# One pace number of a one-core decoder layer: 11 gathered expert rows move from beside the second group's attention and output projection into the expert loop

## The chip, the core and the metric

The program runs on one core of one Trainium2 chip. A core has five engines with a queue each: TensorE (PE in the profile, its weight loads PEld), VectorE (DVE), ScalarE (ACT), GpSimd (POOL) and SyncE (SP). Each works through its own queue in the order in which the instructions stand there, and an instruction that has to wait holds up those behind it. The metric is the device time of one execution, in microseconds (us); lower is better.

## What is computed

One decoder layer on 1024 tokens of width 1024: a mixing half (four retention heads, four heads of causal differential attention, an output projection), then a mixture of 16384 tiny experts (one row of `u` and one of `v` each). Each token picks 128 of them (8 heads, 16 each):

```python
x = x + jnp.concatenate([ret_out, diff_out], axis=-1) @ w_out[l]
x = x + peer(rmsnorm(x, norm_ffn_g[l]), peer_wq[l], peer_subkeys[l], peer_u[l], peer_v[l])
...
# inside peer(), for each block of 128 tokens; e are the 8 x 16 chosen experts of a token, g their gates
ue = jnp.take(u, e, axis=0)
ve = jnp.take(v, e, axis=0)
act = jax.nn.gelu(jnp.einsum('thkd,td->thk', ue, xb), approximate=False)
return jnp.einsum('thk,thkd->td', g * act, ve)
```

## The kernel before

**Two groups of tokens.** The 1024 tokens are eight tiles of 128. Tiles 0 to 2 are the first group ("gathered": `GROUPS[0]`), tiles 3 to 7 the second ("dense"). Both go through `front`: projections, retention and attention by head, output projection, the expert router. Then the experts are done in two ways.

**The dense way**, for the five tiles of the second group: every token meets all 16384 experts. A loop over 32 groups `g` of 4 blocks `e` of 128 experts takes the products with `u` (`experts_in`, lines 740 to 742, PSUM tiles `psH`), GELU, the multiplication by the gates (line 830), the split of the result into a high and a low half (`wh` line 834 on ScalarE, `wl` line 836 on VectorE), the split of `v` (`vh` line 840, `vl` line 842), and the products with `v` (lines 818 to 820). Ten output pieces (tile, half) are summed: four stay in PSUM for the whole loop (`kp0` to `kp3`), six come out of two rotating banks `psV` once a group and are added by VectorE (line 854, `accl`, `accd`, `accS`, `accc_intra`, `accab`, `accpack`, in this order). The `u` products of 39 of the 128 blocks (`SPILL`) are made earlier, beside the router, and stored. After the loop each dense tile is finished: lines 862 and 864 bring its halves together, `finish` squares (line 799, ScalarE), takes the root, and scales (line 801, `fin`).

**The gathered way**, for the three tiles of the first group: per tile 128 rows of `u` (one expert for each token, line 891, an indirect DMA issued by GpSimd into a buffer `ug`), each multiplied with the tokens and summed by VectorE (line 893); then GELU and gates (`shs`, lines 894 and 895); then 128 rows of `v` (line 898, buffer `vg`), each scaled and added into `sa` by VectorE (line 900); then `finish` (`sfin`). That makes 768 rows. The first tile has 5 buffers, which a gather may only refill when VectorE is through with the row that is in it; the later tiles have 7 (line 884 and on, `row`).

**What sets the order.** The gathered rows are written last in the program. A scheduler that models time while it builds puts each engine's queue together, and would take the rows wherever VectorE looks free. `gate` ties the n-th row's VectorE step behind an instruction of the list `gates`; the list is filled by `gated`, which adds `PER` entries (1.5 here) at every step of the generator that it paces:

```python
def gated(g, per):
    due = 0.0
    for y in g:
        due += per[y == "turned"]
        while due >= 1.0:
            gates.append(last_dve())
            due -= 1.0
        yield y
...
run(gated(weave(until(gd, "routing"), sparse_routes(sp, lates, s0, sn, ug, ug, ug), ROUTE, 1), PER[:2]))
```

The paced stretch is the second group's attention with retention, its output projection and the norm behind it, up to the mark "routing". Its 83 steps give 124 entries. Beside the second router and the building of the dense gates (`dense_routes`) `PER[2]` is 0 and no row is let in. The last entry is added at the first gate multiplication (line 830) of the loop: all other rows are free from there on.

Of the kernel before, what the change touches and what calls it, by code (L numbers as in the profile page):

```python
# [56 lines left out]
SPILL = 39  # L57
PACE = (8, 3)
SLOW = 4
PER = (1.5, 1.5, 0.0)  # L60
NC2 = 80
TC = {"schedule_with_timeline_sim": True}

# [36 lines left out]
def layer_kernel(ctx, tc, x, wt, wn, wo, wq, sk, ut, u, v, gmix, gffn, gfin, gsub, dlam, consts, alb, out):  # L100
# [450 lines left out]
    def sparse_routes(rp, late, g0, nt, *rooms):  # L551

        gates_of(rp, late, nt, rooms[0])
        for lt in range(nt):
            t = ST.index(g0 + lt)
            V.tensor_copy(gA[t].rearrange("p (h k) -> p h k", h=PH), late.cv[:, lt])
            i1, i2 = decode(rp, late, lt, *rooms)
            V.scalar_tensor_tensor(i1, i1, float(NK), i2, op0=ALU.mult, op1=ALU.add)
            V.tensor_copy(idxA[t].rearrange("p (h k) -> p h k", h=PH), i1)
            yield  # L560

    def dense_routes(rp, gp, pp, late):

        before = None
        gates_of(rp, late, ND, ("mz", 1))
        for t in range(ND):
            i1, i2 = decode(rp, late, t)
            ps = pp.tile([P, 4, P], F32, tag="B", bufs=2, name="psR")
            for c, src in enumerate((i2, i1, late.cv[:, t])):
                PE.transpose(ps[:, c], src.rearrange("p h k -> p (h k)"), ident)  # L570
            r = rp.tile([P, P // 8, 4, 8], F16, tag="rt", bufs=2, name="rt")
            by = ps.rearrange("p c (q t) -> p q c t", t=8)
            A.activation(r[:, :, 0:2], by[:, :, 0:2], AF.Copy)
            A.activation(r[:, :, 2], by[:, :, 2], AF.Copy, scale=GS)
            V.scalar_tensor_tensor(r[:, :, 3], by[:, :, 2], GS, r[:, :, 2], op0=ALU.mult, op1=ALU.subtract)
            lo = rp.tile([P, P // 8, 8], F32, tag="rl", bufs=2, name="rl")
            if ACTS:
                A.activation(lo, r[:, :, 3], AF.Copy)
            if before is not None:
                yield from build_g(gp, pp, *before)  # L580
            else:
                yield
            before = r, lo, t
        yield from build_g(gp, pp, *before)
# [82 lines left out]
    def pool(name, es=ctx, **kw):  # L667
        return es.enter_context(tc.tile_pool(name=name, bufs=1, reuse_waits="tile", **kw))

    def weave(a, b, na=1, nb=1):  # L670

        i = j = 0
        while a is not None or b is not None:
            if b is None or (a is not None and i * nb <= j * na):
                i += 1
                try:
                    yield next(a)
                except StopIteration:
                    a = None
            else:  # L680
                j += 1
                try:
                    yield next(b)
                except StopIteration:
                    b = None
# [7 lines left out]
# [10 lines that stand above are left out]
    def run(g):  # L703
        for _ in g:
            pass

    def until(g, mark):
        for y in g:
            if y == mark:
                return  # L710
            yield y
# [36 lines left out]
    def spills(pf):  # L748
        for i, ei in enumerate(early):
            two = pf.tile([P, 2, 512], F32, tag="A", bufs=2, name="psHs")  # L750
            SY.dma_start(hs_d[i], experts_in(ei, lambda hf: two[:, hf]))
            yield

    with ExitStack() as es:
# [19 lines left out]
        with ExitStack() as e2:  # L774
            fd = pool("fd", e2)
            md.tp = md.ap = md.fp = fd
            md.big = (fd, "big", BIGS)
            run(gated(weave(until(gd, "routing"), sparse_routes(sp, lates, s0, sn, ug, ug, ug), ROUTE, 1), PER[:2]))
            gh = spills(pf)
            run(weave(gd, islice(gh, 16 // SLOW), SLOW, 1))  # L780
        gp = pool("gp", es)
        run(gated(weave(dense_routes(gp, gp, pf, late), gh, *PACE), (PER[2], 0)))

# [156 lines left out]
```

## Time and profile before

| | us |
|---|---|
| median of 3 runs (2809.43 to 2814.86) | 2811.94 |
| the profiled execution, whole | 2812.24 |
| its span, first to last instruction | 2810.5 |
| around the span | 1.7 |

| stretch of the span | us | what runs |
|---|---|---|
| second group's attention with rows beside it | 445 to 680 | head 0 to 3 |
| output projection, norm, rows beside it | 680 to 803 | |
| router, dense gates, 39 early blocks | 803 to 1260 | no rows |
| change to the loop | 1260 to 1296 | |
| expert loop, with all other rows | 1296 to 2803 | 32 groups |
| last finishes | to 2810.5 | |

A timeline row gives the start, the duration, engine and line, the operation with output and inputs, and in brackets how long the engine had been idle and what ended that. The stretches were taken from the rows of the trace; the busy time of the engines in them is the first group of rows below.

### The profile page before, as it was taken

The page shows a single profiled execution, that of the slowest core. Times are in us where ns is not written, and L with a number is a line of the kernel's source. Part 1 is how long each engine was busy: PE and PEld are TensorE (multiplying, and loading weights), DVE is VectorE, ACT ScalarE, POOL GpSimd, SP SyncE. Part 2 cuts the span into 40 slices and gives each one's busy share as a digit, 9 for nine tenths or more (in the row PEclk, how much of TensorE's full clock was granted, in tenths as well). Part 3 has the DMA queues.
Part 4 walks back from the last instruction along what each step waited for, and adds up shares of the span by engine and source line. Part 5 has one row for each costly group of instructions (what it writes and reads, how often), then busy time and mean ns, then how long its engine had stood idle before and what let it go on. Part 6 is the DMA issues. An engine that isn't in the chain of part 4 may idle for free.

```text
span 2810.5 us, 43147 instructions
## 1 busy us (share of the span) xinstructions
PE 2681.3 (95%) x16043; PEld 2421.6 (86%) x16043; DVE 2303.7 (82%) x4496; ACT 997.4 (35%) x1879; POOL 1071.4 (38%) x782
## 2 busy tenths in 40 slices
PE   7979989888889999999999999999999999999998
PEld 6867888776789999998888888999999999899997
DVE  3554789887478989986999998888998889889987
ACT  4553335554233356772222222222222222223222
POOL 0000004543310000003555556665666567765662
PEclk9989999999989999999999999999999999999999
DMA  7546557877853347799999899898999989989995
GB/s 265 188 177 231 194 191 254 292 276 259 305 193 132 112 150 244 240 281 330 347 347 338 337 374 354 325 348 336 327 344 338 341 333 346 352 317 341 337 348 204
DMA packets 302076, 797.46 MB, mean 284 GB/s; under 512 B 25116, under 2 KB 119336, under 8 KB 297768
## 3 DMA queue, kind: packets, MB, share of 16 engines
q1 hardware_dynamic: 190120, 390.41, 39.2%
q0 software_dynamic: 111744, 404.28, 39.0%
q8 instruction: 126, 2.06, 0.3%
q14 instruction: 86, 0.70, 0.1%
HBM read 698.97 MB, written 95.62 MB: 283 GB/s over the span
## 4 chain that ended last, share of the span: by engine, by line
PE 66%; DVE 8%; DMA 5%; issue 4%; POOL 2%; ACT 1%; SPq 0%; POOLq 0%; DVEq 0%; ACTq 0%
PE psH L742 7%; PE psH L741 7%; PE psH L740 7%; PE psV L818 5%; PE psV L819 5%; PE psV L820 5%; PE kp L820 3%; PE kp L819 3%; PE kp L818 3%; PE psHs L740 3%; PE psHs L742 3%; PE psHs L741 3%; PE psG L613 3%; DVE ug L893 2%; DMA ug<-in_u,idx 2%
## 5 line engine op out<-in xcount | busy, mean ns | idle before, releaser
L891 POOL DMA_INDIRECT ug<-in_u,idx x384 | 529.9, 1380 | 903.5 <-ACT st L615 458.0
L898 POOL DMA_INDIRECT vg<-in_v,idx x384 | 536.1, 1396 | 393.8 <-DVE sa L900 289.8
L893 DVE SCALAR_TENSOR_TENSOR ug<-ug,sx 128x1024 f32<-128x1024 f32 x384 | 458.7, 1223 | 55.5 <-DMA ug<-in_u,idx 54.7
L900 DVE SCALAR_TENSOR_TENSOR sa<-vg,shs,sa 128x1024 f32<-128x1024 f32 x384 | 492.0, 1281 | 10.5 <-DMA vg<-in_v,idx 6.2
L741 PE MATMUL psH<-nl,uh 128*128 128x320 f32 x1424 | 439.5, 309 | 0.0
L740 PE MATMUL psH<-nh,uh 128*128 128x320 f32 x1424 | 439.3, 309 | 0.0
L742 PE MATMUL psH<-nh,ul 128*128 128x320 f32 x1424 | 438.3, 309 | 0.3 <-DVE ul L728 0.3
L818 PE MATMUL psV<-vh,wh 128*128 128x512 f32 x768 | 300.0, 392 | 1.1 <-DVE accl L854 1.1
L819 PE MATMUL psV<-vl,wh 128*128 128x512 f32 x768 | 299.8, 391 | 0.0
L740 PEld LDWEIGHTS psH<-nh,uh 128*128 128x128 f32 x1424 | 267.3, 188 | 5.8
L741 PEld LDWEIGHTS psH<-nl,uh 128*128 128x128 f32 x1424 | 267.3, 188 | 4.8
L742 PEld LDWEIGHTS psH<-nh,ul 128*128 128x128 f32 x1424 | 267.0, 188 | 4.3 <-DVE ul L728 0.6
L726 ACT ACTIVATE uh<-uraw 128x1024 fp32r<-128x1024 f32 x128 | 135.8, 1061 | 321.5 <-PE psH L741 218.0
L743 ACT ACTIVATE ga<-psH 128x320 f32<-128x320 f32 x178 | 75.1, 429 | 447.0 <-PE psH L742 434.2
L740 PE MATMUL psHs<-nh,uh 128*128 128x320 f32 x624 | 195.7, 315 | 6.8 <-ACT ga L743 6.8
L819 PE MATMUL kp<-vl,wh 128*128 128x512 f32 x512 | 200.1, 393 | 0.3 <-DVE vl L842 0.3
L818 PE MATMUL kp<-vh,wh 128*128 128x512 f32 x512 | 194.7, 393 | 4.7 <-ACT wh L834 4.7
L164 ACT ACTIVATE whi<-wraw 128x1024 fp32r<-128x1024 f32 x104 | 109.9, 1058 | 241.2 <-PE psT L173 124.8
L741 PE MATMUL psHs<-nl,uh 128*128 128x320 f32 x624 | 194.1, 311 | 0.0
L742 PE MATMUL psHs<-nh,ul 128*128 128x320 f32 x624 | 192.6, 313 | 0.8 <-DVE ul L728 0.8
L728 DVE TENSOR_TENSOR ul<-uraw,uh 128x1024 fp32r<-128x1024 f32 x128 | 156.9, 1226 | 44.1 <-ACT uh L726 43.9
L820 PE MATMUL psV<-vh,wl 128*128 128x512 f32 x456 | 173.3, 389 | 0.0
(251 smaller groups left out, 6036.4 us busy)
## 6 DMA issues: line engine op xcount, KB each, us to landing
uraw<-in_ut SPq DMA_DIRECT2D x128, 512.0 KB, 6.6
vraw<-in_v SPq DMA_DIRECT2D x128, 512.0 KB, 6.9
g_d<-st SPq DMA_DIRECT2D x80, 512.0 KB, 6.3
gt<-g_d SPq DMA_DIRECT2D x32, 1280.0 KB, 9.6
wl_d<-wlo SPq DMA_DIRECT2D x52, 512.0 KB, 2.9
wlo<-wl_d SPq DMA_DIRECT2D x52, 512.0 KB, 4.3
wraw<-in_wt SPq DMA_DIRECT2D x32, 512.0 KB, 4.4
wraw<-in_wq SPq DMA_DIRECT2D x32, 512.0 KB, 4.6
```

Of the source, the lines that this page charges most:

```text
L726: A.activation(uh, raw, AF.Copy)
L728: V.tensor_sub(ul, raw, uh.bitcast(F32))
L740: PE.matmul(ps, uh[:, dc], xh[:, dc, sl], start=(dc == 0), stop=False)
L741: PE.matmul(ps, uh[:, dc], xl[:, dc, sl], start=False, stop=False)
L742: PE.matmul(ps, ul[:, dc], xh[:, dc, sl], start=False, stop=(dc == DC - 1))
L818: PE.matmul(ps, Wh[e][:, sl], Vh[e][:, so], start=start, stop=False)
L819: PE.matmul(ps, Wh[e][:, sl], Vl[e][:, so], start=False, stop=False)
L820: PE.matmul(ps, Wl[e][:, sl], Vh[e][:, so], start=False, stop=stop)
L891: G.indirect_dma_start(out=ug, out_offset=None, in_=u, in_offset=bass.IndirectOffsetOnAxis(ap=idxA[t][:, k:k + 1], axis=0))
L893: gate(V.scalar_tensor_tensor(ug, ug, 1.0, xt, op0=ALU.mult, op1=ALU.mult, accum_out=hs[:, k:k + 1]))
L898: G.indirect_dma_start(out=vg, out_offset=None, in_=v, in_offset=bass.IndirectOffsetOnAxis(ap=idxA[t][:, k:k + 1], axis=0))
L900: gate(V.scalar_tensor_tensor(ac, vg, hs[:, k:k + 1], ac, op0=ALU.mult, op1=ALU.add))
```

## The change

```diff
-PER = (1.5, 1.5, 0.0)
+PER = (1.37, 1.37, 0.0)
```

The 83 steps now give 113 entries. In VectorE's queue 113 rows, not 124, stand ahead of the loop's first line 830, so the first tile enters the loop with 15 rows of `u` left, not 4. No instruction is added, removed or changed; every queue holds the same instructions in another order. The order is the same up to the first head of the second group, and again, on VectorE and TensorE, through the router and the dense gates. It differs in the paced stretch and in the loop.

In the names below a number belongs to a buffer; `qT`, `kT`, `psT` and so on are as in the code. First place: VectorE beside the attention of the second group, about the end of its first head, as one piece of the difference (- before, + after). `Z` are row maxima and sums, `rz` reciprocals, `am` the masked retention scores, `S` the retention state.

```order
 L893 SCALAR_TENSOR_TENSOR ug,shs<-ug,sx 128x1024
 L371 TENSOR_REDUCE Z<-psS 128x1
-L893 SCALAR_TENSOR_TENSOR ug,shs<-ug,sx 128x1024
 L306 SCALAR_TENSOR_TENSOR S<-S,ret 128x128
-L893 SCALAR_TENSOR_TENSOR ug,shs<-ug,sx 128x1024 x2
-L295 TENSOR_TENSOR am<-ret,c_intra 128x128
-L893 SCALAR_TENSOR_TENSOR ug,shs<-ug,sx 128x1024
-L383 RECIPROCAL rz<-Z 128x1
-L893 SCALAR_TENSOR_TENSOR ug,shs<-ug,sx 128x1024
+L893 SCALAR_TENSOR_TENSOR ug,shs<-ug,sx 128x1024 x3
+L295 TENSOR_TENSOR am<-ret,c_intra 128x128
+L893 SCALAR_TENSOR_TENSOR ug,shs<-ug,sx 128x1024
```

Single rows are taken out or close up. Between the sixth line 382 of the group (of twenty) and the first scaling behind the heads (line 415) 68 rows stand before and 59 after; the other two rows go from the projection and norm behind it.

Second place: VectorE at the start of the loop. Before:

```order
L830 TENSOR_TENSOR gl<-gl,gt 128x640
L893 SCALAR_TENSOR_TENSOR ug,shs<-ug,sx 128x1024 x2
L728 TENSOR_TENSOR ul<-uraw,uh 128x1024
L893 SCALAR_TENSOR_TENSOR ug,shs<-ug,sx 128x1024 x2
L836 TENSOR_TENSOR wls<-gl,wh 128x640
L830 TENSOR_TENSOR gl<-gl,gt 128x640
L895 TENSOR_TENSOR shs<-shs,gA_83 128x128
L900 SCALAR_TENSOR_TENSOR sa<-vg,shs,sa 128x1024
L836 TENSOR_TENSOR wls<-gl,wh 128x640
L900 SCALAR_TENSOR_TENSOR sa<-vg,shs,sa 128x1024
L830 TENSOR_TENSOR ga<-ga,gt 128x640
```

After:

```order
L830 TENSOR_TENSOR gl<-gl,gt 128x640
L893 SCALAR_TENSOR_TENSOR ug,shs<-ug,sx 128x1024 x2
L728 TENSOR_TENSOR ul<-uraw,uh 128x1024
L893 SCALAR_TENSOR_TENSOR ug,shs<-ug,sx 128x1024 x3
L836 TENSOR_TENSOR wls<-gl,wh 128x640
L830 TENSOR_TENSOR gl<-gl,gt 128x640
L893 SCALAR_TENSOR_TENSOR ug,shs<-ug,sx 128x1024 x3
L836 TENSOR_TENSOR wls<-gl,wh 128x640
L893 SCALAR_TENSOR_TENSOR ug,shs<-ug,sx 128x1024 x2
L830 TENSOR_TENSOR gl<-gl,gt 128x640
L830 TENSOR_TENSOR ga<-ga,gt 128x640
L893 SCALAR_TENSOR_TENSOR ug,shs<-ug,sx 128x1024 x2
```

Before, four rows of `u`, then rows of `v`, stand around the first `wl` splits (line 836); after, five rows of `u` stand ahead of the first, three more ahead of the second, four more ahead of the third, and three more ahead of `shs`, behind which all rows of `v` stand.

Third place: VectorE's end, from the last `wl` split of the loop on. Before:

```order
L836 TENSOR_TENSOR wl_13178<-ga,wh 128x640
L900 SCALAR_TENSOR_TENSOR sa<-vg,shs,sa 128x1024 x2
L137 RECIPROCAL rs_f<-rs_f 128x1
L801 SCALAR_TENSOR_TENSOR sfin<-sa,rs_f,gfb 128x1024
L862 TENSOR_TENSOR fa<-kp_13170,fa 128x512
L862 TENSOR_TENSOR fa<-kp_13171,fa 128x512
L854 TENSOR_TENSOR accl<-psV,accl 128x512
L854 TENSOR_TENSOR accd<-psV,accd 128x512
```

After, the beginning and the end of it:

```order
L836 TENSOR_TENSOR wl_13178<-ga,wh 128x640
L900 SCALAR_TENSOR_TENSOR sa<-vg,shs,sa 128x1024 x4
L862 TENSOR_TENSOR fa<-kp_13170,fa 128x512
L862 TENSOR_TENSOR fa<-kp_13171,fa 128x512
L854 TENSOR_TENSOR accl<-psV,accl 128x512
L900 SCALAR_TENSOR_TENSOR sa<-vg,shs,sa 128x1024
L854 TENSOR_TENSOR accd<-psV,accd 128x512
...
L137 RECIPROCAL rs_f<-rs_f 128x1
L900 SCALAR_TENSOR_TENSOR sa<-vg,shs,sa 128x1024
L801 SCALAR_TENSOR_TENSOR fin<-fa,rs_f,gfb 128x1024
L137 RECIPROCAL rs_f<-rs_f 128x1
L801 SCALAR_TENSOR_TENSOR sfin<-sa,rs_f,gfb 128x1024
```

Before, 2 rows are left there and `sfin` of the third tile comes ahead of all dense finishes. After, 15 rows are left (4 and then 11 singly between the lines 854, 862, 864 and 801), and `sfin` is the last instruction of the queue. Between the first line 830 and this place 642 rows stand before, 640 after.

## Rows read from the trace of the kernel before

**Rows 1.** Busy us (and instructions) of each engine, clock and DMA by stretch.

```profile
core 0: us, PE busy (x) PEld busy (x) DVE busy (x) ACT busy (x) POOL busy (x), PEclk, DMA share, GB/s
...
505.00:680.00 175.00, 151.28 (x961) 130.10 (x960) 143.97 (x274) 89.37 (x235) 83.80 (x72) 0.94 0.76 266
...
1380.00:2760.00 1380.00, 1377.01 (x7472) 1237.32 (x7472) 1224.55 (x1461) 352.56 (x492) 850.61 (x597) 1.00 0.92 341
```

**Rows 2.** VectorE's timeline: the combining step L382 of the shortest tile, four heads.

```profile
447.03 0.77 DVE L382 SCALAR_TENSOR_TENSOR e<-e,rz,e 128x512 f32<-128x512 f32 x1
...
508.33 0.75 DVE L382 SCALAR_TENSOR_TENSOR e<-e,rz,e 128x512 f32<-128x512 f32 x1
...
574.35 0.75 DVE L382 SCALAR_TENSOR_TENSOR e<-e,rz,e 128x512 f32<-128x512 f32 x1
...
634.48 0.75 DVE L382 SCALAR_TENSOR_TENSOR e<-e,rz,e 128x512 f32<-128x512 f32 x1
```

**Rows 3.** Waits from 505 to 680 us: total us, times, longest.

```profile
DVE ug L893 <- DMA ug<-in_u,idx: 19.9, 15, 2.9
...
PE ret L297 <- DVE am L295: 7.3, 4, 3.4
PE pov L393 <- DMA dvh<-dv_d: 5.8, 1, 5.8
```

**Rows 4.** VectorE's timeline at the loop's start: start, us, instruction, idle before.

```profile
1296.66 0.83 DVE L830 TENSOR_TENSOR gl<-gl,gt 128x640 f32<-128x640 f32 x1 [5.65 <-issue]
...
1298.55 1.22 DVE L893 SCALAR_TENSOR_TENSOR ug<-ug,sx 128x1024 f32<-128x1024 f32 x1
...
1303.12 0.82 DVE L836 TENSOR_TENSOR wls<-gl,wh 128x640 fp32r<-128x640 f32 x1
...
1306.12 0.82 DVE L836 TENSOR_TENSOR wls<-gl,wh 128x640 fp32r<-128x640 f32 x1
1306.85 1.28 DVE L900 SCALAR_TENSOR_TENSOR sa<-vg,shs,sa 128x1024 f32<-128x1024 f32 x1
...
1320.44 1.28 DVE L900 SCALAR_TENSOR_TENSOR sa<-vg,shs,sa 128x1024 f32<-128x1024 f32 x1 [2.22 <-DMA vg<-in_v,idx]
1321.64 0.68 DVE L854 TENSOR_TENSOR accl<-psV,accl 128x512 f32<-128x512 f32 x1
```

**Rows 5.** GpSimd's timeline: gathers ahead of the loop and in its first 15 us.

```profile
1260.01 0.94 POOL L891 DMA_INDIRECT ug<-in_u,idx  x1 [457.97 <-ACT st L615]
...
1298.90 1.68 POOL L898 DMA_INDIRECT vg<-in_v,idx  x1 [36.71 <-DVE ug L893]
...
1311.18 1.43 POOL L898 DMA_INDIRECT vg<-in_v,idx  x1 [0.30 <-issue]
```

**Rows 6.** TensorE's timeline at the loop's start: expert 1's last products; third psV.

```profile
1308.35 0.62 PE L820 MATMUL kp<-vh,wls 128*128 128x512 f32 x2
...
1324.63 0.39 PE L818 MATMUL psV<-vh,wh 128*128 128x512 f32 x1
```

**Rows 7.** VectorE's timeline at the end of the program.

```profile
2741.94 2.60 DVE L900 SCALAR_TENSOR_TENSOR sa<-vg,shs,sa 128x1024 f32<-128x1024 f32 x2
2744.45 0.68 DVE L854 TENSOR_TENSOR accc_intra<-psV,accc_intra 128x512 f32<-128x512 f32 x1
...
2779.64 2.60 DVE L900 SCALAR_TENSOR_TENSOR sa<-vg,shs,sa 128x1024 f32<-128x1024 f32 x2
...
2785.50 1.28 DVE L801 SCALAR_TENSOR_TENSOR sfin<-sa,rs_f,gfb 128x1024 f32<-128x1024 f32 x1 [0.27 <-DVE rs_f L137]
2786.70 1.28 DVE L862 TENSOR_TENSOR fa<-kp,fa 128x512 f32<-128x512 f32 x2
...
2803.31 0.43 DVE L864 COPY fa<-accpack 128x512 f32<-128x512 f32 x1
2805.28 0.17 DVE L137 RECIPROCAL rs_f<-rs_f 128x1 f32<-128x1 f32 x1 [1.54 <-ACT rs_f L136]
2805.48 1.28 DVE L801 SCALAR_TENSOR_TENSOR fin<-fa,rs_f,gfb 128x1024 f32<-128x1024 f32 x1
```

**Rows 8.** TensorE's timeline: the last products of kp0 and kp1.

```profile
2785.38 0.62 PE L820 MATMUL kp<-vh,wl 128*128 128x512 f32 x2
```

## The prediction

> **What bounds the kernel now.** I read the busy time by stretch first, then the waits inside the paced stretch, then VectorE's timeline at the two ends of the loop, because the change touches only VectorE's work and its order.
>
> In the loop TensorE is busy in 1377.0 of 1380 us, VectorE in 1224.6 [rows 1]. TensorE sets the pace there and VectorE has 155 us to spare. In the second group's attention neither is full: from 505 to 680 us TensorE is busy in 151.3 of 175 us, at a mean granted clock of 0.94, which is mostly the upper of its two levels, and VectorE in 144.0 [rows 1]. They alternate: VectorE stands 19.9 us still for gathered rows that have not landed, TensorE 7.3 us for the masked scores that VectorE makes, and 5.8 us for a load of `dvh` that has nothing to do with the rows [rows 3]. At the end of the program the last dense `fin` starts at 2805.48 and takes 1.28, so VectorE ends at 2806.8 [rows 7]; the rest of the span is the last store.
>
> So the change takes VectorE work out of a stretch in which VectorE matters in part, and adds it to one where it mostly doesn't. What it costs is decided by where in the loop the rows stand, and the order says: not in the 155 us. Up to the last `wl` split the loop holds 642 rows before and 640 after. The excess stands at its two ends.
>
> **The change, part by part.** The sum goes against the profiled execution, 2812.2 us, which is 0.3 above the median of the runs, so the two are taken as one.
>
> *The end: dearer by 10.* When the last `wl` split is through, at 2779.64, VectorE has 2 rows left before and 15 after, among the dense finishes. The first is set by TensorE through `ga`, so it stays where it is against TensorE. Two rows and the next start lie 2.51 us apart (2741.94 to 2744.45), 1.25 a row [rows 7]. What VectorE does there besides rows: four L862 at 0.64, six L854 at 0.65 (0.68 less an overlap), six finishing scalings at 1.2 (2785.50 to 2786.70), and six copies and six reciprocals, which take 0.43 and 0.17 each but overlap, some 2.5 in all [rows 7]. That is 16.2; with 15 rows, 18.8, it is 35.0 us of work. Two waits stay: four rows end at 2784.6, and L862 needs `kp0` and `kp1`, whose last products end at 2785.38 + 0.62 = 2786.0 [rows 8], so 1.4; and the last row must be squared and rooted on ScalarE ahead of the very last `sfin` (1.54 of waiting for the last `fin` before [rows 7]), less the 1.2 of a `fin` that lies between, so 0.4. 2779.6 + 35.0 + 1.4 + 0.4 = 2816.4, against 2806.8 some 10. Gathers don't hold it: 15 rows in 36 us are 2.4 us each, and GpSimd issues one in 1.7 and 0.3 behind it [rows 5]. The ends: 13 rows more at 1.25 are 16.3, and of VectorE's last 27 us before only 18.7 are work (16.2 and two rows), so 8 if all of its idle time is filled, 12 if half of it.
>
> *The start: dearer by 4.5.* Before, the first `wl` splits start at 1303.12 and 1306.12, with four rows of `u` ahead that were gathered long before [rows 4]. After, a fifth row stands ahead of the first split: 1.2 later (one L893 [rows 4]), and TensorE, which waits for just that split, with it. Ahead of the second split stand three rows whose gathers can only be issued once the first buffers are free, from 1298.90 on, some 2 us apart [rows 5]. Issue to use was 8.0 us for the first of them before (1298.90 to 1306.85, without a wait), and 9.3 for one that VectorE did wait for (1311.18 to 1320.44, 2.22 of it waiting) [rows 4, 5]. So the third of them is there at about 1311 and the split ends at about 1312.5. TensorE wants it at 1308.35 [rows 6] plus 1.2: a stall of up to 3. Seven more rows, at the same two us each, stand ahead of `shs` and of the first `accl` addition, which was at 1321.64 [rows 4] and would come at about 1331; TensorE's third `psV`, at 1324.63 before [rows 6], needs that bank. By this TensorE is 6.6 late; if a gather lands in 6 us instead of 8, the stalls shrink to about 2. I take 4.5, nearer to the 8.0 that the row shows, less a little that TensorE's waits in the next group can swallow. Ends 2 and 7. The sixth row's gather is queued on GpSimd behind two gathers of the next tile; those go out from 1260.01 on [rows 5], ahead of the loop, so they hold nothing up.
>
> *The attention and the projection: cheaper by 6.5.* Nine rows leave the heads (68 to 59), two the projection and norm. The upper end: if VectorE's queue paces the heads, each of the nine is worth its 1.22 [rows 4] and its share of the waits for rows, 19.9 / 68 = 0.3 [rows 3], and the other two 1.2 each, so 16. The lower end: if TensorE paces them, the time of a head doesn't depend on the rows. Heads begin 61.3, 66.0 and 60.1 us apart with 28, 24 and 22 rows among them [rows 2]; without the 5.8 us of the `dvh` wait in the second they are 61.3, 60.2 and 60.1. Six rows more go with 1.2 us more, 0.2 a row, so 2. The stretch has 23.7 us in which TensorE idles [rows 1], and outside the wait for `dvh` that is 18 at most for VectorE to answer for; nine of 68 rows, in proportion, give 2.4 of them and a little of the lost clock. The rows stand nearer to the lower end, but the marginal row costs more than the mean one when a buffer is short. I take 5.5 for the heads and 1 for what follows, where VectorE waits for TensorE and DMA more than for its own work. Reordering alone may turn this by some us either way, so the lower end goes to zero.
>
> Router and dense gates have no rows and the same order: nothing. DMA carries the same bytes.
>
> Sum: 2812.2 + 10 + 4.5 - 6.5 = 2820.2.
>
> [...]
>
> **The rivals.**
> *The loop takes them free*: TensorE's queue hides both ends, as the 155 us of room would let it. Then only the gain is left, 2812.2 - 6.5 = 2805.7, faster. Against it: the last 13 rows stand behind TensorE's last needs, where nothing hides them.
> *VectorE's queue paces the heads in full*: gain 16, start 4.5 and end 10 as above, 2810.7, no change. This is the one on the other side. Its place is 505 to 680 us, its price 1.5 us a row, and it decides from a stretch that is shorter by 12 or more. For it: VectorE's 144.0 busy and 19.9 waiting leave little of 175. Against it: the even heads.
> *Rows are free in the heads, and the start costs its upper end*: gain 2, start 6.5, end 10, 2826.7, slower.
> *The change doesn't do what it says* is out: the queues show the rows moved.
>
> **How the numbers follow.** The forecast, 2814 to 2825 around 2820, has 0.52; the even rival (2807 to 2814) 0.23; the dear one (2825 to 2829) 0.15; the free one (2803 to 2807) 0.07; 0.03 lies outside. 0.2% is 5.6 us, about what a measurement of this kernel can tell from no change: faster is under 2806.3, slower over 2817.6. Of the forecast's own chance some 0.4 lies above 2817.6, with the dear rival and half of what is outside 0.57. The even rival and the rest of the forecast give 0.35, the free one and the remainder 0.08. The range 2808 to 2828 leaves out the free rival, the fastest part of the even one and a sliver at the top, some 0.15 together.
>
> **What would show it.** Right: `sfin` is VectorE's last instruction, some 14 us after TensorE's last product instead of dense `fin` 4 us after it; the second `wl` split ends near 1312 against a loop start at 1296.7 (15 us in, not 10); the start of the loop's first line 830 is 4 to 9 us earlier. Wrong: that start 12 or more us earlier (the even rival), or not earlier at all (the dear one); TensorE without a new wait in the loop's first 40 us (the start term falls); the distance from TensorE's last product to the end unchanged (the end term falls, and the free rival holds).

## The result: 27.8 us slower

The changed kernel takes 2839.89 us (median of 4 runs, 2836.37 to 2840.85) against 2812.1 us for the kernel before on the same chip: a ratio of 1.009, with a 95% interval of 1.0074 to 1.0107. Forecast were 2820 us, and 2828 at most. The sign was right, the size was not, and the reason is not the one that the forecast gave.

The spans of the two profiled executions, 2839.1 and 2810.5 us, differ by 28.6 us. Three marks split them: the loop's first L830 on VectorE, TensorE's last product, and the end of VectorE's last step. (TensorE's first product with `v` starts 1.65 us behind that L830 in both kernels, so the three rows add up.)

| stretch | before | after | difference | forecast |
|---|---|---|---|---|
| up to the loop's first L830 | 1296.66 | 1316.94 | +20.3 | -6.5 |
| loop, TensorE's first product with `v` to its last | 1503.85 | 1504.05 | +0.2 | +4.5 |
| TensorE's last product to VectorE's last step | 4.21 | 12.31 | +8.1 | +10 |

Of the +20.3, L415 (the end of the second group's attention, 695.47 before, 708.64 after) shows +13.2, the last L444 (the end of projection and norm) +17.5. So the loss lies where rows were taken away. The busy time by stretch (columns: window, its length, then busy us and instructions of PE, its weight load, DVE, ACT and POOL, granted clock, DMA share, GB/s), the attention from the same step to L415, first the kernel before:

```profile
508.00:695.00 187.00, 162.15 (x1004) 138.73 (x1003) 147.93 (x292) 92.49 (x239) 84.36 (x72) 0.95 0.78 277
```

And the kernel after, the stretch that answers to it, and the fixed one of [rows 1]:

```profile
508.00:709.00 201.00, 169.79 (x1017) 145.32 (x1016) 138.25 (x276) 93.80 (x244) 78.41 (x64) 0.92 0.68 235
...
505.00:680.00 175.00, 147.55 (x930) 127.78 (x929) 127.78 (x246) 83.75 (x224) 72.87 (x61) 0.93 0.68 231
```

VectorE lost 9.7 us of work, as meant, and the stretch is 14 us longer. TensorE's idle time rose from 24.9 to 31.2 us, and its busy time by 7.6 us for nearly the same products: the mean granted clock fell from 0.95 to 0.92. The heads, which began 61.3, 66.0 and 60.1 us apart [rows 2], now begin like this (VectorE's timeline, L382 of the shortest tile; start, us), 64.4 and 70.4 us apart, with 65.5 us from the last to L415 (61.0 before). So 10.2 of the 13.2 us lie in the head from 572.82 on:

```profile
508.39 0.75 DVE L382 SCALAR_TENSOR_TENSOR e<-e,rz,e 128x512 f32<-128x512 f32 x1
...
572.82 0.75 DVE L382 SCALAR_TENSOR_TENSOR e<-e,rz,e 128x512 f32<-128x512 f32 x1
...
643.18 0.74 DVE L382 SCALAR_TENSOR_TENSOR e<-e,rz,e 128x512 f32<-128x512 f32 x1
```

TensorE's waits (us in total, times, longest) in this stretch: the waits for `am` and `dvh` [rows 3] shrank, and two others grew most. Before, the wait for `rv` was

```profile
PE ret L293 <- ACT rv L312: 2.4, 4, 1.1
```

and TensorE had no wait for `pt` of L320. After:

```profile
PE ret L293 <- ACT rv L312: 7.2, 3, 4.5
PE ret L297 <- DVE am L295: 4.0, 3, 2.3
PE psT L172 <- ACT pt L320: 4.0, 1, 4.0
```

The timeline of all engines around the longest shows the whole chain (start, us, engine, line; in brackets the idle time before it and what ended it):

```profile
577.12 1.23 DVE L893 SCALAR_TENSOR_TENSOR ug<-ug,sx 128x1024 f32<-128x1024 f32 x1 [2.82 <-DMA ug<-in_u,idx]
...
577.35 0.31 PE L173 MATMUL psT<-hl,whi 128*128 128x320 f32 x1
...
580.45 1.23 DVE L893 SCALAR_TENSOR_TENSOR ug<-ug,sx 128x1024 f32<-128x1024 f32 x1 [2.09 <-DMA ug<-in_u,idx]
...
581.60 0.28 DVE L306 SCALAR_TENSOR_TENSOR S<-S,ret 128x128 f32<-128x128 f32 x1
...
581.98 0.37 ACT L310 ACTIVATE jk<-ret,c_cross 128x128 bf16<-128x128 f32 x1 [7.25 <-DVE S L306]
...
582.34 0.36 ACT L312 ACTIVATE rv<-ret,c_cross 128x128 f32<-128x128 f32 x1
...
582.75 0.58 PE L293 MATMUL ret<-qT,kT 128*128 128x128 f32 x1 [4.50 <-ACT rv L312]
```

It is read from the bottom. TensorE waits 4.50 us for ScalarE's `rv`, which stands behind `jk`; `jk` waits 7.25 us for VectorE's `S`, the retention's state step of 0.28 us; and `S` is late since two gathered rows stand ahead of it on VectorE's queue, whose data land only at 577.12 and 580.45, while the product that `S` adds (L304) ended at 576.6. VectorE stood idle in both waits. In the kernel before one row stands between the same L382 (574.35 [rows 2]) and this `S`, and TensorE had no such wait:

```profile
576.87 1.23 DVE L893 SCALAR_TENSOR_TENSOR ug<-ug,sx 128x1024 f32<-128x1024 f32 x1 [1.77 <-DMA ug<-in_u,idx]
...
578.76 0.28 DVE L306 SCALAR_TENSOR_TENSOR S<-S,ret 128x128 f32<-128x128 f32 x1
```

The wait for `pt`, in the same head, has the same form with another short step: a late row stands ahead of `qb` (L325, L326) on VectorE, and ScalarE's next `pt` waits for `qb`.

```profile
619.46 1.23 DVE L893 SCALAR_TENSOR_TENSOR ug<-ug,sx 128x1024 f32<-128x1024 f32 x1 [3.05 <-DMA ug<-in_u,idx]
...
621.23 0.49 DVE L326 TENSOR_TENSOR qb<-pt,qa 64x320 fp32r<-64x320 f32 x1
...
621.75 0.44 ACT L320 ACTIVATE pt<-psT 128x320 f32<-128x320 f32 x1 [4.10 <-DVE qb L326]
...
622.24 0.41 PE L172 MATMUL psT<-hh,whi 128*128 128x320 f32 x1 [3.98 <-ACT pt L320]
```

Behind the first of the two stalls TensorE runs slower for a while: the clock (last but two column) by ten microseconds,

```profile
565.00:575.00 10.00, 9.32 (x69) 8.70 (x69) 9.11 (x17) 4.62 (x13) 4.55 (x3) 1.00 0.74 268
575.00:585.00 10.00, 5.03 (x31) 4.49 (x30) 5.79 (x10) 3.02 (x7) 3.68 (x3) 0.87 0.78 240
585.00:595.00 10.00, 10.00 (x60) 9.21 (x60) 5.81 (x13) 3.73 (x12) 4.22 (x5) 0.79 0.76 268
```

where the kernel before has 1.00 in all three windows; and a `psT` product, which took 0.31 us at 577, takes 0.47 at 585:

```profile
585.25 0.47 PE L173 MATMUL psT<-hl,whi 128*128 128x320 f32 x1
```

Read in windows of one microsecond from 505 to 680, the clock is 1.00 in 152 and 0.50 in 17 of the 175 of the kernel before, 1.00 in 146 and 0.50 in 19 of the changed one; the few others lie between, at the edges of the low stretches. These are the two levels that the prediction speaks of, and a mean such as 0.79 is one over both. Behind this stall the clock is 0.50 from 583 to 589. So the stall shows twice in the trace, as 4.50 us of idle time and as products of 0.47 us instead of 0.31 behind it.

At the end the last rows do what the forecast said: TensorE's last product starts at 2822.64 (2802.16 before), and `sfin` follows a dense `fin` as VectorE's last step, where `fin` was last before [rows 7]:

```profile
2831.03 1.28 DVE L900 SCALAR_TENSOR_TENSOR sa<-vg,shs,sa 128x1024 f32<-128x1024 f32 x1
2832.24 1.28 DVE L801 SCALAR_TENSOR_TENSOR fin<-fa,rs_f,gfb 128x1024 f32<-128x1024 f32 x1
2833.86 0.16 DVE L137 RECIPROCAL rs_f<-rs_f 128x1 f32<-128x1 f32 x1 [0.35 <-ACT rs_f L136]
2834.06 1.28 DVE L801 SCALAR_TENSOR_TENSOR sfin<-sa,rs_f,gfb 128x1024 f32<-128x1024 f32 x1
```

And at the loop's start the first `wl` split comes 7.7 us behind the first L830 (1316.94), the second 13.5, where they came 6.5 and 9.5 behind it [rows 4]. TensorE waits there for that first split (2.37 us, 0.20 before) and for `accl` (0.85, none before):

```profile
1324.62 0.81 DVE L836 TENSOR_TENSOR wls<-gl,wh 128x640 fp32r<-128x640 f32 x1
...
1330.48 0.82 DVE L836 TENSOR_TENSOR wls<-gl,wh 128x640 fp32r<-128x640 f32 x1
...
1348.37 0.69 DVE L854 TENSOR_TENSOR accl<-psV,accl 128x512 f32<-128x512 f32 x1
```

### The profile page after: what moved, and what is told of

It is laid out like the page before. It is cut to its first block, busy times and chain, and to the rows that moved or that the text cites. A ratio compares the mean times of both kernels' runs of the same rounds, so it can differ in the third digit from the quotient of the medians.

```text
span 2839.1 us, 43152 instructions
## 1 busy us (share of the span) xinstructions
PE 2688.6 (95%) x16043; PEld 2429.5 (86%) x16043; DVE 2304.3 (81%) x4496; ACT 995.8 (35%) x1879; POOL 1079.7 (38%) x782
## 4 chain that ended last, share of the span: by engine, by line
PE 71%; DVE 7%; issue 3%; DMA 3%; ACT 1%; POOL 0%; DVEq 0%; SPq 0%; ACTq 0%; POOLq 0%
PE psH L742 7%; PE psH L741 7%; PE psH L740 7%; PE psV L818 6%; PE psV L819 6%; PE psV L820 6%; PE kp L819 4%; PE kp L820 4%; PE kp L818 4%; PE psHs L740 3%; PE psHs L742 3%; PE psHs L741 3%; PE psG L613 3%; PE psT L172 2%; PE psT L173 2%
## 5 line engine op out<-in xcount | busy, mean ns | idle before, releaser
L891 POOL DMA_INDIRECT ug<-in_u,idx x384 | 536.4, 1397 | 958.9 <-ACT st L615 460.7
```

The source lines that it names most:

```text
L891: G.indirect_dma_start(out=ug, out_offset=None, in_=u, in_offset=bass.IndirectOffsetOnAxis(ap=idxA[t][:, k:k + 1], axis=0))
```

## The experiments

The table gives all runs: rows on VectorE up to L415, ahead of the loop, and behind the loop's last `wl` split (counted in VectorE's queue); the time's ratio to the kernel before with its interval; from the profiles the difference to before at L415 and at the loop's first L830, the loop from TensorE's first product with `v` to its last, and from there to VectorE's end. (e7 and e8 have two runs each.)

| kernel | rows | ratio (95%) | L415 | loop's start | loop | end |
|---|---|---|---|---|---|---|
| before | 96 / 124 / 2 | 1 | 0 | 0 | 1503.9 | 4.2 |
| after | 87 / 113 / 15 | 1.0090 (1.0074 to 1.0107) | +13.2 | +20.3 | 1504.1 | 12.3 |
| e1 | 89 / 124 / 2 | 1.0080 (1.0056 to 1.0104) | +10.4 | +26.0 | 1503.6 | 4.2 |
| e2 | 93 / 113 / 13 | 1.0015 (1.0004 to 1.0025) | -2.7 | -8.1 | 1503.9 | 12.0 |
| e3 | 87 / 113 / 2 | 1.0073 (1.0050 to 1.0097) | +13.5 | +19.5 | 1505.6 | 4.2 |
| e4 | 91 / 118 / 9 | 1.0026 (1.0009 to 1.0044) | -2.6 | -1.4 | 1510.8 | 7.2 |
| e5 | 87 / 113 / 15 | 1.0102 (1.0074 to 1.0129) | +14.9 | +17.9 | 1505.8 | 12.3 |
| e6 | 102 / 132 / 0 | 1.0050 (1.0032 to 1.0068) | +7.3 | +15.2 | 1506.2 | 6.5 |
| e7 | 83 / 107 / 21 | 1.0174 (1.0143 to 1.0205) | +19.0 | +23.1 | 1513.2 | 23.2 |
| e8 | 64 / 83 / 43 | 1.0141 (1.0110 to 1.0172) | -7.9 | -12.0 | 1509.0 | 54.2 |
| e9 | 87 / 113 / 14 | 1.0000 (0.9987 to 1.0013) | -16.3 | -11.8 | 1506.3 | 11.5 |
| e10 | 96 / 124 / 2 | 1.0016 (1.0001 to 1.0031) | +2.7 | +4.3 | 1504.4 | 4.2 |
| e11 | 88 / 119 / 8 | 1.0011 (1.0000 to 1.0022) | -12.9 | -5.5 | 1509.2 | 5.5 |
| e12 | 91 / 118 / 9 | 0.9986 (0.9972 to 1.0001) | -14.6 | -11.8 | 1511.8 | 7.2 |

**Each half of the change alone.** In e1 the pace is 1.37 up to the last head and 1.812 from the projection on, so that the loop gets its 124 rows back; in e2 it is 1.5 in the heads and 1.05 from the projection on, so that only the later rows move.

```
         due = 0.0
+        pace = per
         for y in g:
-            due += per[y == "turned"]
+            if y == "mixed" and per[0]:
+                pace = PER2          # (1.812, 1.812) in e1, (1.05, 1.05) in e2
+            due += pace[y == "turned"]
```

> The changed pace (1.37) only up to the end of the heads; from there 1.81, so that 124 rows stand ahead of the loop as before. Through the heads the queues are those of the changed kernel (87 to 89 rows, not 96), the start of the loop and the end of the program are those of before (2 rows left behind the last wl split). Theory A, the new order of the queues in the heads is itself the loss (there the changed kernel lost 8 us by the last line 382 and 13 by the first line 415), and the ends of the loop cost some 10 more: about 2812 + 13 = 2825, range 2821 to 2832, and the last dense fin is the last instruction again. Rival B, the whole loss hangs on the rows that the loop takes: about 2812.

> The pace of before (1.5) through the heads, and 1.05 behind them, so that 113 rows stand ahead of the loop as in the changed kernel. Through the heads the queues are those of before; the loop starts with 15 rows of u left and ends with 13 rows behind the last wl split. Theory A: the heads as before (line 415 first reached at 695 give or take 3), the end dearer by 7 to 8 and the start of the loop by 0 to 3, less 0 to 3 for the rows gone behind the heads: 2812 + 8 = 2820, range 2815 to 2824. Rival B: 2836 to 2840, as the changed kernel. Rival C, fewer rows anywhere ahead of the router lengthen that stretch: 2826 or more.

2836.44 and 2816.55 us; e1 lies above its range by 4 us, e2 in it. With the loop as before, e1 keeps nearly the whole loss: it sits in the heads and, in e1, in a projection that now takes more rows. The two stalls of the changed kernel are in e1 again, 4.40 us for `rv` and 4.03 for `pt`, as in e3 below, 3.62 and 4.23. The rows that leave the projection (e2) bring 5.4 us between L415 and the loop, and the end takes 7.8 of them back. The loop itself costs nothing in either. Rival B, that the whole loss hangs on the rows that the loop takes, missed both.

**The end without its rows.** e3 is the changed kernel without the last 13 rows of `v` of the third tile.

```
-        for k in range(HK):
+        for k in range(HK - 13 if t == NS - 1 else HK):
             vg = row(t, HK + k, "vg")
```

> The changed kernel with the last 13 rows of v of the third tile left out (115 of 128 are added), so that 2 rows stand behind the last wl split as before; heads, projection and the start of the loop as in the changed kernel. If the rows behind the last split cost what the traces show (the last dense fin 28.6 late, of which 20.5 are there at the last line 830), 2840 - 8 = 2832, range 2829 to 2834. If TensorE sets the end anyway, 2839 to 2841.

2833.84 us, in the range, and VectorE ends 4.2 us behind TensorE's last product, to a hundredth as before. The end term is real and is VectorE's work alone.

**Is it the number of rows?** e4, e6, e7 and e8 change only `PER`, to 1.43, 1.6, 1.3 and 1.0.

> The pace 1.43 throughout: 118 rows ahead of the loop, 91 up to line 415, 9 behind the last wl split. Theory A says that the heads' length goes by where rows fall in the queue, not by their number: anywhere from 0 to 14 us against before, plus 4 to 6 at the end, so 2816 to 2832. If the loss grew evenly with the number of rows moved (28 us for 11), 6 rows would be 15 us: 2827.

> Before with PER 1.6: 102 rows up to L415, 132 ahead of the loop, none left behind the loop's last expert. Theory N (the prediction's price: each row in the heads and projection costs the stretch about 0.6 us, each row behind the loop's last expert about 0.7 us): the paced stretch lengthens by some 5 us, the end gains 0 to 1.5 us, 2815 to 2818 us. Theory A (what counts is which steps stand behind rows that have not landed; the pace sets it without order): the stretch may come out anywhere from 5 us shorter to 20 us longer, and the profile shows TensorE's waits of over 2 us with a gathered row as the last cause where it is longer. Start of the loop by both: within 3 us of the kernel before.

> PER 1.3: 83 rows up to L415, 107 ahead of the loop, 21 left behind the loop's last expert. Theory N: the paced stretch 10 us shorter than the kernel before (17 rows fewer at 0.6 us), the end 13 to 16 us longer, 2815 to 2820 us. Theory A: the paced stretch between 5 us shorter and 20 us longer, not in line with 1.37 (+13 at L415) and 1.43 (-3); the end 13 to 16 us longer; 2818 to 2848 us.

> PER 1.0: 64 rows up to L415, 83 ahead of the loop, 43 left behind the loop's last expert. With a third fewer rows they have more time to land, so both theories expect a shorter paced stretch: by theory N 20 to 25 us shorter than the kernel before (41 rows fewer at 0.6 us), by theory A 5 to 20 us. The end takes 43 rows at 1.23 us each less what it has room for (some 8 us): 35 to 45 us longer. In all 2825 to 2850 us. A stretch no shorter than before's would say that the rows cost the heads nothing at all and that the loss is elsewhere.

2821.65, 2829.34, 2864.01 and 2854.83 us. Theory N missed e6 and e7 and, by its stretch, e8; the even price per row missed e4. Theory A's ranges, which are wide, hold e4's time and the stretches of e6 to e8, but the times of e7 and e8 lie above both theories: the end took 19.0 and 50.0 us more than before, where 13 to 16 and 35 to 45 were expected, and e7's loop 9.3 more. No price per row fits L415: 102, 96, 91, 87, 83 and 64 rows give +7.3, 0, -2.6, +13.2, +19.0 and -7.9 us. Even 32 rows fewer gain only 7.9, 0.25 us a row. The waits tell more than the number. In e7, with 83 rows, the chain of the changed kernel is there again, at another head, behind five rows (timeline of all engines, as above):

```profile
685.57 1.23 DVE L893 SCALAR_TENSOR_TENSOR ug<-ug,sx 128x1024 f32<-128x1024 f32 x1 [3.50 <-DMA ug<-in_u,idx]
...
692.17 1.23 DVE L893 SCALAR_TENSOR_TENSOR ug<-ug,sx 128x1024 f32<-128x1024 f32 x1 [2.91 <-DMA ug<-in_u,idx]
...
693.32 0.28 DVE L306 SCALAR_TENSOR_TENSOR S<-S,ret 128x128 f32<-128x128 f32 x1
...
693.64 0.37 ACT L310 ACTIVATE jk<-ret,c_cross 128x128 bf16<-128x128 f32 x1 [5.73 <-DVE S L306]
...
694.40 0.80 PE L293 MATMUL ret<-qT,kT 128*128 128x128 f32 x2 [4.39 <-ACT rv L312]
```

In e6, with more rows than before, it is `am` that stands behind them: four rows, of which the first waits 5.49 us, and a wait of 9.02 us on TensorE. The other three had landed; their own 1.2 us each is part of that wait.

```profile
625.04 1.23 DVE L893 SCALAR_TENSOR_TENSOR ug<-ug,sx 128x1024 f32<-128x1024 f32 x1 [5.49 <-DMA ug<-in_u,idx]
...
632.65 0.28 DVE L295 TENSOR_TENSOR am<-ret,c_intra 128x128 f32<-128x128 f32 x1
```

```profile
632.98 0.47 PE L297 MATMUL ret<-pack,kT 128*128 128x128 f32 x1 [9.02 <-DVE am L295]
```

What the runs do give is a price of the end: 0, 2, 8, 9, 13 to 15, 21 and 43 rows left give 6.5, 4.2, 5.5, 7.2, 12, 23.2 and 54.2 us. Some eight rows find room; beyond 15 each costs 1.8, then 1.4 us.

**One row moved.** e5 is the changed kernel with one entry of the gates' list replaced, so that one row fewer stands ahead of the `S` that TensorE waited for. (Lines behind the edit count 2 more there, as they count 1 more in e9, e10 and e12.)

```
+    for a, b in [(46, 47)]:
+        gates[a] = gates[b]
```

> The changed kernel with one entry of the gates' list edited: gates[46] = gates[47], so that one row fewer stands on VectorE's queue ahead of the retention's state step (S, L306) of the head in which TensorE waited 4.50 us in the changed kernel's profile (from 582.75 us, for ret L293, behind ScalarE's rv L312, which waited for S). In the changed kernel two gathered rows, landing at 577.12 and 580.45, stand between the softmax's L382 and that S; here one does, as in the kernel before. All other rows, 113 ahead of the loop and 15 behind its last expert, stay. Theory A (rows that have not landed, standing ahead of a step for which TensorE waits, are the loss): the stretch from the 23rd to the 25th L382 (574 to 601 us) shortens by 4 to 6 us against the changed kernel and its wait of 4.50 us falls below 1.5 us; the later losses (weights of the projection, end of the program) stay, so about 2834 us in all, 2831 to 2837. Theory B (the loss comes from fewer rows as such): the order of one row does nothing, 2838 to 2841 us.

2843.1 us: theory A's number was missed, and so was its stretch from the 23rd to the 25th L382, 28.4 us where the changed kernel has 28.8. TensorE's wait of 4.50 us was gone, and its `psT` products, which take 0.47 us from 584.45 on in the changed kernel, still took 0.31 at 583.15. But `S` came as late as before: the one row ahead of it waited 5.41 us. TensorE had other products in its queue there (busy 9.78 of the 10 us from 575 on). So a late row ahead of `S` is not enough; TensorE's own order at that moment decides whether it has to wait.

```profile
580.48 1.23 DVE L895 SCALAR_TENSOR_TENSOR ug<-ug,sx 128x1024 f32<-128x1024 f32 x1 [5.41 <-DMA ug<-in_u,idx]
...
581.63 0.28 DVE L306 SCALAR_TENSOR_TENSOR S<-S,ret 128x128 f32<-128x128 f32 x1
```

Counted from head to head, a gain and a loss show: this head took 66.4 us instead of 70.4, the last one 70.6 instead of 65.5. The scheduler had set the rows behind the edit anew, and the same chain stood one head later:

```profile
680.94 1.23 DVE L895 SCALAR_TENSOR_TENSOR ug<-ug,sx 128x1024 f32<-128x1024 f32 x1 [3.92 <-DMA ug<-in_u,idx]
...
684.67 0.28 DVE L306 SCALAR_TENSOR_TENSOR S<-S,ret 128x128 f32<-128x128 f32 x1
...
684.99 0.37 ACT L310 ACTIVATE jk<-ret,c_cross 128x128 bf16<-128x128 f32 x1 [4.71 <-DVE S L306]
...
685.76 0.79 PE L293 MATMUL ret<-qT,kT 128*128 128x128 f32 x2 [4.54 <-ACT rv L312]
```

One place could be mended, not the mechanism. So the next edit takes ScalarE's link out of the chain, whatever stands where.

**The link taken out.** `jk` reads another part of the same bank as `S`, and in the traces the one that is issued later waits for the other: `jk` for `S` in the kernels so far (7.25 us in the chain above). e9 (the change) and e10 (before) issue `S` behind the two ScalarE steps; there `S` waits for `rv`, in e9 twice and 2.1 us in all.

```
+                jk = ap.tile(...)
+                A.activation(jk, bank[:, 2], AF.Square, ...)
+                A.activation(vt, bank[:, 2], AF.Copy, ...)
                 if tg < NT - 1:
                     if tg:
                         V.scalar_tensor_tensor(S[:, h], ...)
...
-                jk = ap.tile(...)
-                A.activation(jk, bank[:, 2], AF.Square, ...)
-                A.activation(vt, bank[:, 2], AF.Copy, ...)
```

> The changed kernel with the retention's state step S (L306 on VectorE) issued behind the two ScalarE steps that read the same bank (jk L310, rv L312) and no longer ahead of them. In the kernels so far jk waits for S (the program's order of the two readers of one PSUM bank), so that a row that has not landed, ahead of S on VectorE's queue, holds ScalarE's rv and with it the next head's first product on TensorE (ret L293). Rows and pace stay. Theory A (this chain, rows - S - jk - rv - ret, is the loss in the heads): the waits of ret L293 for rv fall from 7 us to under 2 us in the stretch up to L415, that stretch shortens by 6 to 13 us against the changed kernel, 2827 to 2834 us in all. Theory B (the loss is in the number of rows, the weights' transfers or the clock by itself): less than 3 us change, 2837 to 2842 us.

> The same edit in the kernel before. There ret L293 waits for rv only 2.5 us in this stretch, so theory A expects little: 0 to 5 us less, 2807 to 2815 us, and the distance between this kernel and the one before it in the list (the change with the same edit) shrinks from 28 us to 12 to 22 us, of which 8 to 10 us are the end of the program. Theory B: the distance stays at 25 to 30 us.

2813.08 and 2816.94 us: 14 us below the range for e9, 2 above it for e10. The change with this edit is 26.8 us faster than without it (25 by the ratios in the table), the kernel before gains nothing from it, and the distance between the two, expected at 12 to 22 us, is 4 the other way (the end of the program, 7.3 us dearer, included). So the number of rows is not the loss: e9 has the changed kernel's 87 rows up to L415, and the loss is gone. The attention of e9 in the columns of above, 175.3 us from the same step to L415 instead of 200.2, with a clock of 0.97:

```profile
504.00:679.00 175.00, 154.57 (x987) 133.48 (x986) 132.16 (x263) 91.53 (x234) 76.09 (x59) 0.97 0.74 253
```

The rows still wait for their data, in e9 26.4 us in all, more than in the changed kernel (18.5 up to L415). At the step where the changed kernel has its long stall, e9 has two late rows ahead of `S` as well:

```profile
559.58 1.23 DVE L894 SCALAR_TENSOR_TENSOR ug<-ug,sx 128x1024 f32<-128x1024 f32 x1 [2.10 <-DMA ug<-in_u,idx]
...
559.91 0.37 ACT L306 ACTIVATE jk<-ret,c_cross 128x128 bf16<-128x128 f32 x1 [2.30 <-PE ret L304]
...
563.82 1.23 DVE L894 SCALAR_TENSOR_TENSOR ug<-ug,sx 128x1024 f32<-128x1024 f32 x1 [3.01 <-DMA ug<-in_u,idx]
...
564.97 0.28 DVE L311 SCALAR_TENSOR_TENSOR S<-S,ret 128x128 f32<-128x128 f32 x1
...
565.31 0.77 PE L293 MATMUL ret<-qT,kT 128*128 128x128 f32 x2 [3.89 <-DVE S L311]
```

ScalarE no longer stands still: `jk`, `rv` and what it prepares behind them run ahead of `S`. But TensorE still waits for the bank, now for `S` itself, 3.89 us where it was 4.50 (in e10 four such waits, 9.5 us in all), and from the L382 ahead of this place to the second one behind it 4.2 us are gained, 24.6 instead of 28.8. That is a sixth of the 24.9. The edit changed more than the link: the first L382 of the group comes 11.8 us earlier than in the changed kernel, before any row is let in, the second head takes 52.1 us instead of 64.4 though no long wait for `S` or `rv` stood there, and TensorE's waits for `dvh` (3.7 us) and for `pt` (4.0) are gone too or under 1 us. What the ScalarE link is worth by itself these two runs don't tell.

Over all runs the link goes with the length only roughly. `jk` waited for `S` in this stretch 12.9 us before, 11.6 in e2 and 12.8 in e4, the three short ones with 90 or more rows; 18.6 in the changed kernel, 16.3 in e1, 20.7 in e5, 16.0 in e7; in e9 and e10 never, of which e10 is long all the same. (e6 has 14.0 and its long wait for `am`; e8 is short in spite of 16.6, with 64 rows.)

**Towards a faster one.** e11 is e9 with 1.6 from the projection on, e12 is e9 with `PER` 1.43.

> The state step behind ScalarE's two steps, the changed kernel's 1.37 up to the last head (the queues there are those of e9), and 1.6 from the projection on: 88 rows up to L415, 119 ahead of the loop, 8 left behind the loop's last expert instead of 14. Theory A (heads set by what stands behind unlanded rows; the end costs some 7 us with 14 rows left and 2 to 3 us with 8 or 9): L415 12 to 16 us earlier than in the kernel before, as in e9; the projection up to the last L444 takes back 2 to 5 us; the end 4 to 5 us cheaper than in e9; 2807 to 2814 us. If only the number of rows counted (theory N), the five rows more would cost the projection 3 us and the end gain 4 us: 2811 to 2815 us.

> The state step behind ScalarE's two steps, and PER 1.43: 91 rows up to L415, 118 ahead of the loop, 9 left. Against e4 (the same pace with the state step ahead; there the wait of ret L293 for rv was 1.6 us only, no long one), theory A expects no gain of the size seen between the changed kernel and e9 (27 us): within 12 us of e4's 2821.65, 2805 to 2822 us. If the edit of the state step were a gain by itself, whatever the order of the rows, it would be 20 us or more here too: 2795 to 2802 us.

2815.68 and 2811.4 us. e11 nearly keeps e9's attention and saves 6 us at the end, where 4 to 5 were expected, but loses 6 ahead of the loop and 3 in it; its number was missed by 2 us. e12 has the shortest attention but one and is the fastest of all by its median, yet its interval reaches 1.0001: it beats the changed kernel by 28 us, and the kernel before by nothing that these runs can tell. Against e4, the same pace with `S` ahead, it is 10 us faster, within theory A's range.

## Why the forecast was too low

- **The heads, -5.5 forecast, +13.2 measured: the failed step.** (With projection and router the term was -6.5, and measured +20.3.) It priced a row, between 0.2 us (TensorE paces) and 1.5 us (VectorE paces), and took a value between. Both ends assumed that fewer rows are never dearer. The forecast saw VectorE's waits for rows [rows 3] as time that goes with the rows, 0.3 us each, and set the reordering at "some us either way", bounded at zero. But VectorE works through its queue in order, as the trace shows: two rows whose data landed at 577.12 and 580.45 held `S` behind them until 581.60, 5.0 us after its product had ended. What stands behind a late row is decided by the scheduler anew for each pace. With nine rows fewer, two late rows came to stand ahead of an `S` and one ahead of a `qb`, and through ScalarE TensorE stood still for 4.50 and 3.98 us, in the head that grew by 10.2. The traces show both chains, in e1 and e3 at the same places too; e4 to e9 show that the number of rows is not the cause. No run took one chain out and left the rest as it was, so how the 13.2 us divide between the stalls, the clock and the rest of the new order is not shown. A single price per row does not hold either: 0.25 us a row over 32 rows (e8), and no order in between.
- **The clock** was in the forecast only as "a little of the lost clock" to be gained. It fell behind the first new stall (0.79 from 585 to 595), and TensorE is busy 7.6 us longer up to L415 (162.15 to 169.79), about half of the loss there.
- **Projection and router, part of the same term:** -1 forecast, +7 from L415 to the loop. TensorE's waits for the weights `wlo` grew there (4.0 to 5.9 us up to the last L444) and the clock fell (0.88 to 0.86). In e2, with the heads as before and eight rows fewer behind them, this stretch gained 5.4 us, 0.7 a row, near the forecast's 0.5. Why the changed kernel loses there was not settled; e9, with the same rows, loses 4.6 in it as well.
- **The start of the loop, +4.5 forecast, +0.2 net.** The mechanism was right: the first split 1.2 us later (6.5 to 7.7), the second ending at 14.4 us where 15 were said, the first `accl` addition at 31.4 us instead of 34, and TensorE's two new waits, 3.2 us. But by its last product the loop had given that back: over the whole loop TensorE idles 1.7 us longer and is busy 1.5 us less. Why it is busy less is not shown. The first rival's idea, that the loop takes the rows free, holds for this term: the loop as a whole took 1504.05 us with two rows fewer and another start against 1503.85. It isn't general: with 118 rows ahead of the loop (e4, e12) the loop took 7 and 8 us more.
- **The end, +10 forecast, +8.1 measured.** Right in mechanism and place; `sfin` is VectorE's last instruction and ends 12.3 us behind TensorE's last product, where 14 were said and a dense `fin` ended 4.2 behind it before. Of the 13 rows more about six found room among the finishes, so the lower end of that term, 8, was the better choice. e3 confirms it.
- **The rivals** all shared the failed step: each had the heads gain 2 to 16 us. The sign named for the dear one came, the loop's start not earlier at all, but its 2826.7 us is missed too, and not for its reason. The rival that speaks of a wait that takes the place of the one removed was missing.

## What to carry to other kernels

When work that waits for transfers is moved in a queue that issues in order, price it by what stands behind it, not by its own time: look up in the changed order which short step of the slow chain (here a state step of 0.28 us) now follows an instruction whose data are late. Then look at who else is tied to that step, and whether the order of issue can be turned: here two ScalarE steps waited up to 7.25 us for it since they were issued behind it, and none when they were issued ahead. That is worth a run, not a promise: it went with a gain of 26.8 us in one kernel and with none in the other. And look at the queue's order before the pace of such a filler is tuned by number: 96, 91, 87 and 83 rows gave 0, -2.6, +13.2 and +19.0 us, and with `S` issued last 96, 91 and 87 gave +2.7, -14.6 and -16.3.

## What was not expected of the hardware

- A stall of TensorE of 4.5 us was followed by products at 0.47 instead of 0.31 us and a granted clock of 0.79 over the next full ten microseconds, though TensorE was busy all through them.
- The rows left behind TensorE's last product cost 1.4 us each where nothing covers them (31.0 us for 22, e7 to e8), a little above VectorE's 1.25 a row [rows 7].
- Not tried: the changed order with rows whose data have landed already, which would part the order from the waiting.
